# Interleaved products behind the LayerNorms, the conditioning row's Silu in memory, and two squares on VectorE in a two-layer diffusion step

## The chip, the cores and the metric

The kernel runs on one core of a Trainium2 chip. A core has TensorE (PE, the matmuls; PEld are its weight loads), VectorE (DVE), ScalarE (ACT), GpSimd (POOL) and SyncE (SP, which mostly starts DMAs). Each has its own instruction queue and works through it in order; semaphores between the queues hold an instruction back until its operands are there. What counts is the time of one execution on the device, in microseconds (us).

## The reference

Two layers, each a half-step SwiGLU FFN, a token mixer and another half-step FFN; the mixer is neighbourhood attention in layer 0 and a Hyena long convolution in layer 1. There are 640 tokens (128 of context, 512 latent), 1024 channels and 2816 hidden channels in an FFN. Every sub-layer is modulated from a conditioning vector and ends with a LayerNorm:

```
def modulate(x, shift, scale):
    return x * (1.0 + scale) + shift

def swiglu(h, w_in, w_out):
    g, u = jnp.split(h @ w_in, 2, axis=-1)
    return (jax.nn.silu(g) * u) @ w_out

def trunk_layer(x, cond, ...):
    sh1, sc1, g1, ... = jnp.split(jax.nn.silu(cond) @ mod_w_i + mod_b_i, N_MOD, axis=-1)
    x = layer_norm(ALPHA * x + 0.5 * g1 * swiglu(modulate(x, sh1, sc1), ...), ...)
    mix, extras = mixer(modulate(x, sh2, sc2))
    x = layer_norm(ALPHA * x + g2 * mix, ...)
    x = layer_norm(ALPHA * x + 0.5 * g3 * swiglu(modulate(x, sh3, sc3), ...), ...)
```

## The kernel before, in words

The six sub-layers are stages 0 to 5, and each has the LayerNorm of its number at its end: FFN 0, attention, FFN 1, FFN 2, Hyena, FFN 3. So LayerNorm 0 leads to attention, 1 to FFN 1, 2 to FFN 2, 3 to Hyena, 4 to FFN 3, and 5 to the output. x lies in memory with channels on partitions, as eight row blocks (dt or k, 0 to 7) of 128 channels by 640 tokens; the tokens are two chunks, c = 0 and c = 1, of CH = 320.

Products are made in fp32r with every operand split in a high and a low part (xh and xl, wh and wl): a row block takes three matmuls of 320 columns, a product over eight row blocks 24. A chunk's modulated row block is made by ACT (xm, L362), its high part by DVE (L386) or ACT (L388), its low part by DVE (L390).

`norm_steps` is a LayerNorm of one chunk, a generator in four steps: mean over channels by matmuls with a constant (mu, L401 and L403); its copy for POOL (mus, L405); subtraction on DVE, or on POOL for dt 2, 5 and 7 (L411), and squares (sq, L413); their mean (va, L420), square root and reciprocal (rq, L425 and L426) and its spread over partitions (rx, L428); the product that brings it to all rows (rs, L432); and last the multiplication of every row block (L436) with its modulation. The LayerNorm of chunk 0 runs inside the last products of its stage. That of chunk 1 is pending when they end: `tick()`, which the product helpers call after every fourth row block, takes it one step on at the 1st, 3rd, 4th and 6th tick (TICK_IN), and `settle()` finishes it. So the products with which the next stage starts on chunk 0 lie between its steps.

An FFN (`ffn`) starts with its plain products (`do_plain(f, c)`, two for each f: gate z = 0 and value z = 1; FIRST names the first three pairs (f, z)): f = 0 and 1 of chunk 0, then `settle()`, then the same for chunk 1. Each product is emitted whole, row block after row block. Then Silu on ACT (sg, L584), the multiplication (L572) and the split of the hidden row block (hh, hl). All later f are made by `do_fast(f)`, a seven-product scheme on four quarter blocks of the weights, whose sums s1 to s4 (L593 to L596, 128x512) are made on DVE for the first such f of an FFN and on POOL for the others. `combine_blocks` and `combine_rest` make the combined operands t1 to t5 for it from chunks 0 and 1 on DVE and ACT. `rescale` applies a LayerNorm's gain and bias to x on POOL (L477), 16 row blocks behind the first fast ones.

Attention starts with value products v0_5 and v0_0 and the query product qk0_0_0, Hyena with three of its input products, again each product as a whole.

`ffn_scope` loads the conditioning row for each FFN (condw, broadcast to 128 partitions by four DMAs) and applies Silu to it on ACT (L496); DVE uses it (L247) while it makes modulation vectors of later stages out of streamed weights.

Instructions are written in program order, and a scheduler then reorders them per engine by its own model of the times, within the dependences and the pools' buffers; `pin` keeps those that are passed through it in their written order. PSUM is in pools: two banks "mm", one "md", five "f" during an FFN. The name of a tile with its numbers, such as f2_0_0_1, is FFN 2, f = 0, c = 0, z = 1; mu2_1 is the mean of LayerNorm 2, chunk 1; s2_3_0 is the first sum of f = 3 in FFN 2.

## Time and profile before

| | |
|---|---|
| runs, median (lowest to highest) | 2799.68 us (2796.84 to 2804.33), 3 runs |
| the profiled execution | 2800.67 us |
| its span, first to last instruction | 2798.9 us |
| PE busy | 2683.2 us, 96% |
| DVE busy | 2111.8 us, 75% |
| ACT busy | 1196.1 us, 43% |
| POOL busy | 991.4 us, 35% |
| matmuls | 19404 |

The profile is of one execution, whose own time is 1.0 us above the median of the runs; 1.8 us of it lie outside the span. A busy matmul is modelled, and matmuls overlap: one of 320 columns is shown with 0.31 us, and the next one starts 0.15 us later when the clock is at its full level. The granted clock (PEclk) is 1.00 at 2.4 GHz and 0.50 at 1.2 GHz; a value between in a stretch is a mean of the two.

### The profile page before, as it was taken

How to read it: one execution, taken by the hardware profiler on the slowest of the kernel's cores; microseconds unless marked ns; L12 is line 12 of the kernel's file. 1: busy time of each engine (PE TensorE's matmuls, PEld its weight loads, DVE VectorE, ACT ScalarE, POOL GpSimd, SP SyncE). 2: the span in 40 equal slices, each digit the busy share in tenths (PEclk: the TensorE clock that was granted, in tenths of full speed). 3: DMA queues.
4: the chain of work that ended last, by engine and by line, in shares of the span. 5: the costliest groups of instructions: out<-in, count | busy, mean ns of one | idle time of the engine just before them, and what ended most of it. 6: DMA issues, size and time to landing. Idle time of an engine off the chain costs nothing.

```text
span 2798.9 us, 51125 instructions
## 1 busy us (share of the span) xinstructions
PE 2683.2 (96%) x19404; PEld 2558.2 (91%) x19404; DVE 2111.8 (75%) x4778; ACT 1196.1 (43%) x2572; POOL 991.4 (35%) x811
## 2 busy tenths in 40 slices
PE   7999999999999989999999999999999998999998
PEld 6898999989999688999989899998999987999997
DVE  5797888865765688888878888886777777765765
ACT  5662432444444462424346243344433336443433
POOL 4442533440000143534425354344223234543542
PEclk9999999999999999999999999999999998999999
DMA  8623324312222523243231332332423331322321
GB/s 281 236 95 98 126 91 129 114 56 90 77 74 74 191 73 128 84 129 129 84 106 63 112 128 91 121 121 67 132 84 106 101 100 35 99 76 76 98 68 54
DMA packets 111134, 293.45 MB, mean 105 GB/s; under 512 B 13823, under 2 KB 28927, under 8 KB 110760
## 3 DMA queue, kind: packets, MB, share of 16 engines
q1 hardware_dynamic: 107576, 285.80, 31.7%
q0 software_dynamic: 2304, 4.20, 0.5%
q8 instruction: 153, 2.51, 0.4%
q14 instruction: 93, 0.76, 0.1%
q10 hardware_dynamic: 1008, 0.19, 0.1%
HBM read 275.98 MB, written 14.16 MB: 104 GB/s over the span
## 4 chain that ended last, share of the span: by engine, by line
PE 67%; DVE 17%; DMA 6%; issue 4%; ACT 3%; POOL 3%; DVEq 0%; ACTq 0%; POOLq 0%; SPq 0%
PE f L527 8%; PE f L528 8%; PE f L529 8%; PE o L527 5%; PE o L528 5%; PE o L529 5%; DVE junk L247 5%; DMA mh<-in_modt 3%; DVE wl L158 3%; PE hy L343 2%; PE hy L342 2%; PE hy L344 2%; DVE xl L158 2%; PE qk L342 1%; PE qk L343 1%
## 5 line engine op out<-in xcount | busy, mean ns | idle before, releaser
L157 ACT CAST wh<-raw 128x512 fp32r<-128x512 f32 (+1 forms) x327 | 230.4, 709 | 302.5 <-PE o L528 151.9
L158 DVE TENSOR_TENSOR wl<-raw,wh 128x512 fp32r<-128x512 f32 (+1 forms) x274 | 274.6, 1003 | 70.1 <-ACT wh L157 69.3
L527 PE MATMUL f<-xh,wh 128*128 128x320 f32 x956 | 296.3, 314 | 15.7 <-DVE q L606 10.0
L528 PE MATMUL f<-xl,wh 128*128 128x320 f32 x956 | 297.5, 312 | 2.7 <-DVE xl L390 2.7
L529 PE MATMUL f<-xh,wl 128*128 128x320 f32 x956 | 294.7, 311 | 0.0
L247 DVE SCALAR_TENSOR_TENSOR junk<-mh,condw 128x256 f32<-128x256 f32 x576 | 267.1, 510 | 32.2 <-DMA mh<-in_modt 31.4
L527 PE MATMUL o<-hh,wh 128*128 128x320 f32 x840 | 261.0, 314 | 5.2 <-ACT hh L157 5.2
L528 PE MATMUL o<-hl,wh 128*128 128x320 f32 x840 | 259.1, 309 | 0.0
L529 PE MATMUL o<-hh,wl 128*128 128x320 f32 x840 | 258.1, 309 | 0.0
L353 DVE SCALAR_TENSOR_TENSOR x<-o,drv,x 128x320 f32<-128x320 f32 (+2 forms) x384 | 153.8, 434 | 105.3 <-PE o L529 104.7
L158 DVE TENSOR_TENSOR wl<-s,wh 128x512 fp32r<-128x512 f32 x187 | 170.9, 914 | 69.0 <-ACT wh L157 65.5
L157 ACT CAST wh<-s 128x512 fp32r<-128x512 f32 x187 | 115.8, 620 | 228.6 <-POOL s L594 69.3
L527 PE MATMUL f<-xh,xh 128*128 128x320 f32 x628 | 194.6, 314 | 8.1 <-DVE q L606 4.2
L593 POOL TENSOR_TENSOR s<-raw 128x512 f32<-128x512 f32 x73 | 110.7, 1516 | 256.2 <-DVE junk L247 167.3
L527 PEld LDWEIGHTS f<-xh,wh 128*128 128x128 f32 x956 | 180.0, 189 | 21.2 <-DVE q L606 12.1
L528 PE MATMUL f<-xl,xh 128*128 128x320 f32 x628 | 195.0, 311 | 0.2 <-DVE xl L390 0.2
L529 PE MATMUL f<-xh,xl 128*128 128x320 f32 x628 | 193.1, 310 | 0.0
L595 POOL TENSOR_TENSOR s<-raw,raw 128x512 f32<-128x512 f32 x73 | 106.5, 1459 | 238.6 <-DVE wl L158 150.2
L528 PEld LDWEIGHTS f<-xl,wh 128*128 128x128 f32 x956 | 180.8, 189 | 4.7 <-DVE xl L390 4.5
L527 PE MATMUL o<-hh,xh 128*128 128x320 f32 x568 | 178.2, 316 | 3.4 <-ACT hh L157 3.4
L529 PEld LDWEIGHTS f<-xh,wl 128*128 128x128 f32 x956 | 180.6, 189 | 0.0
L528 PE MATMUL o<-hl,xh 128*128 128x320 f32 x568 | 176.7, 312 | 1.2 <-DVE hl L158 1.2
(496 smaller groups left out, 8874.0 us busy)
## 6 DMA issues: line engine op xcount, KB each, us to landing
raw<-in_win SPq DMA_DIRECT2D x176, 512.0 KB, 3.6
raw<-in_wout SPq DMA_DIRECT2D x88, 512.0 KB, 4.3
mh<-in_modt SPq DMA_DIRECT2D x144, 256.0 KB, 2.9
raw<-in_modw SPq DMA_DIRECT2D x62, 512.0 KB, 4.8
raw<-in_hyin SPq DMA_DIRECT2D x24, 512.0 KB, 3.7
ksb<-kspec SPq DMA_DIRECT2D x40, 256.0 KB, 2.7
kspec<-ks SPq DMA_DIRECT2D x32, 256.0 KB, 3.2
raw<-in_wqk SPq DMA_DIRECT2D x16, 512.0 KB, 3.5
```

The source lines that it names most:

```text
L157: act.copy(pair[0], src)
L158: (eng or dve).tensor_tensor(pair[1], src, pair[0], ALU.subtract)
L247: dve.scalar_tensor_tensor(junk, raw[:, 256 * g:256 * g + 256], 1.0, condw[0][:, z], ALU.mult, ALU.mult, accum_out=acc[:, g0 + g, t, z:z + 1])
L342: te.matmul(ps, wh[:, i, cols], kh(k), start=(i == 0), stop=False)
L343: te.matmul(ps, wh[:, i, cols], kl(k), start=False, stop=False)
L344: te.matmul(ps, wl[:, i, cols], kh(k), start=False, stop=(i == n - 1))
L353: dve.scalar_tensor_tensor(x[:, dt, sl], ps[:, o], drv[:, st, 2, dt, z:z + 1], x[:, dt, sl], ALU.mult, ALU.add)
L527: te.matmul(ps, wh, kh, start=(first and i == 0), stop=False, skip_group_check=True)
L528: te.matmul(ps, wh, kl, start=False, stop=False, skip_group_check=True)
L529: te.matmul(ps, wl, kh, start=False, stop=(last and i == n - 1), skip_group_check=True)
L593: eng.tensor_tensor(s1, a21, a22, ALU.add)
L595: eng.tensor_tensor(s3, a11, a21, ALU.subtract)
```

## The change

Five things change. First, `interleaved` emits three products together, row block by row block, each in a bank of its own, with a tick behind every row block (eight ticks instead of two for each product). It is used for the first three products of each chunk in an FFN (`plain_pair` takes the place of `do_plain` for f = 0 and 1; the fourth product of the chunk follows as a whole), for v0_5, v0_0 and qk0_0_0 in attention, and for the first three products of Hyena. Second, the conditioning row gets its Silu once at the start and goes to a DRAM row, condd; `ffn_scope` loads that, and its Silu goes. Third, the squares of dt 6 and 7 are made on DVE. Fourth, banks: the LayerNorm of chunk 1 takes md behind stages 0 and 3, `ln_bank` (va from mm, the rest from md) behind 1, 2 and 4, and f behind 5. Fifth, the sums of the first fast f stay on DVE in FFN 0 only; in FFN 1, 2 and 3 they go to POOL with the others.

```diff
--- before.py
+++ after.py
...
+SQDVE = (6, 7)
...
+    def ln_bank(name):
+        return mm_bank(name) if name.startswith("va") else md_bank(name)
...
+    condd = dr.tile([4, 512], F32, name="condd")
+    crow = tmp("crow", 512, 4)
+    act.dma_start(out=crow, in_=a["condw"])
+    act.activation(crow, crow, AF.Silu)
+    act.dma_start(out=condd, in_=crow)
...
+    def interleaved(items):
+        for k in range(KD):
+            for ps, operands in items:
+                (sh, sl), (mh, ml) = operands(k)
+                for i, (s_, m_) in enumerate(((sh, mh), (sh, ml), (sl, mh))):
+                    te.matmul(ps, s_, m_, start=(k == 0 and i == 0), stop=(k == KD - 1 and i == 2),
+                              skip_group_check=True)
+            tick()
...
-                act.activation(sq, x[:, dt, sl], AF.Square)
+                if dt in SQDVE:
+                    dve.tensor_tensor(sq, x[:, dt, sl], x[:, dt, sl], ALU.mult)
+                else:
+                    act.activation(sq, x[:, dt, sl], AF.Square)
...
-                         in_=a["condw"][q:q + 1].broadcast_to([32, 512]))
-        act.activation(cw, cw, AF.Silu)
+                         in_=condd[q:q + 1].broadcast_to([32, 512]))
...
+            def plain_pair(c):
+                for key in FIRST + ((1, 1),):
+                    if key not in plain:
+                        plain[key] = uget(("win", idx) + key)
+                x_ = xb(range(KD), c)
+                ps = [fbank(f"f{idx}_{f}_{c}_{z}") for f, z in FIRST]
+                interleaved([(b, lambda k, u=plain[key]: (block(u, k), x_[k])) for b, key in zip(ps, FIRST)])
+                ps.append(fbank(f"f{idx}_1_{c}_1"))
+                product(ps[3], plain[(1, 1)], 0, x_)
+                for f in range(2):
+                    sg = tmp(f"sg{idx}_{f}_{c}", CH)
+                    act.activation(sg, ps[2 * f], AF.Silu)
+                    hidden(f, c, sg, ps[2 * f + 1], dve)
...
-                    b = mm_bank(f"f{idx}_{f}_{c}_{z}")[:, :CH] if (idx, f, c) == (0, 0, 0) else fbank(f"f{idx}_{f}_{c}_{z}")
+                    b = fbank(f"f{idx}_{f}_{c}_{z}")
...
-                eng = dve if f == NPLAIN[idx] else pool
+                eng = dve if idx == 0 and f == NPLAIN[idx] else pool
...
-                for f, c in [(0, 0), (1, 0), (0, 1), (1, 1)] + [(f, c) for f in range(2, NPLAIN[idx]) for c in range(2)]:
-                    if (f, c) == (0, 1):
-                        settle()
-                        t3 = combine_blocks(st)
-                    do_plain(f, c)
+                plain_pair(0)
+                settle()
+                t3 = combine_blocks(st)
+                plain_pair(1)
+                for f in range(2, NPLAIN[idx]):
+                    for c in range(2):
+                        do_plain(f, c)
...
-                pending.append(LayerNorm(1, st, md_bank if (st + 1) % 3 == 1 else fbank, nsum, TICK_IN))
+                pending.append(LayerNorm(1, st, fbank if st == 5 else md_bank if st % 3 == 0 else ln_bank, nsum, TICK_IN))
...
-            pending.append(LayerNorm(1, st, bank, nsum, TICK_IN))
+            pending.append(LayerNorm(1, st, ln_bank, nsum, TICK_IN))
...
-            values(0, wv, 5)
-            values(0, wv, 0)
             w0 = qk_slab(0, 0)
-            qk_gemm(0, 0, 0, w0)
...
+            bv = [mm_bank(f"v0_{slot}")[:, :256] for slot in (5, 0)]
+            bq = sc_bank("qk0_0_0")[:, :CH]
+            xh0, xl0 = xkh(0), xkl(0)
+            interleaved([(bv[0], value_operands(0)), (bv[1], value_operands(CTX + HD)),
+                         (bq, lambda k: ([t[:, k, :] for t in w0], (xh0(k), xl0(k))))])
...
-                first = [chunk(item, 0, w, mm_bank if i < 2 else hy_bank) for i, (item, w) in enumerate(head)]
+                first = [(mm_bank if i < 2 else hy_bank)(f"hyf{i}")[:, :CH] for i in range(3)]
+                xh0, xl0 = xkh(0), xkl(0)
+                interleaved([(b, lambda k, w=w: ([t[:, k] for t in w], (xh0(k), xl0(k))))
+                             for b, (_, w) in zip(first, head)])
```

Three places of the resulting order, all behind LayerNorm 2. PE, the first products of FFN 2, before; f2_0_0_0 is the product for f = 0, chunk 0, z = 0, s1_1 the sum over row blocks that the mean starts from:

```order
L527 MATMUL f2_0_0_0_16565<-xh_112,wh0_102 128x320
L528 MATMUL f2_0_0_0_16565<-xl_113,wh0_102 128x320
L529 MATMUL f2_0_0_0_16565<-xh_112,wl0_103 128x320
L527 MATMUL f2_0_0_0_16565<-xh_112,wh0_102 128x320
L528 MATMUL f2_0_0_0_16565<-xl_113,wh0_102 128x320
L529 MATMUL f2_0_0_0_16565<-xh_112,wl0_103 128x320
L401 MATMUL mu2_1_16578<-s1_1_115,mean_w_83 128x320
L403 MATMUL mu2_1_16578<-x_111,mean_w_83 128x320
L527 MATMUL f2_0_0_0_16565<-xh_112,wh0_102 128x320
L527 MATMUL f2_0_0_1_16607<-xh_112,wh1_104 128x320
```

The same place on PE now:

```order
L381 MATMUL f2_0_0_0_16573<-xh_117,wh0_107 128x320
L381 MATMUL f2_0_0_1_16574<-xh_117,wh1_109 128x320
L381 MATMUL f2_0_0_0_16573<-xl_118,wh0_107 128x320
L381 MATMUL f2_0_0_0_16573<-xh_117,wl0_108 128x320
L381 MATMUL f2_0_0_1_16574<-xl_118,wh1_109 128x320
L381 MATMUL f2_0_0_1_16574<-xh_117,wl1_110 128x320
L381 MATMUL f2_0_0_0_16573<-xh_117,wh0_107 128x320
L381 MATMUL f2_0_0_1_16574<-xh_117,wh1_109 128x320
L381 MATMUL f2_1_0_0_16575<-xh_117,wh2_111 128x320
L381 MATMUL f2_1_0_0_16575<-xl_118,wh2_111 128x320
L381 MATMUL f2_1_0_0_16575<-xh_117,wl2_112 128x320
L419 MATMUL mu2_1_16585<-s1_1_120,mean_w_83 128x320
```

Before, one product had PE for four row blocks, then came mu2_1, then the rest of the product. Now two, then three products share a row block, and the first of mu2_1's passes stands between matmuls of the second row block.

DVE at the end of chunk 0's chain, before; xm_5_0 to xm_7_0 are modulated row blocks, s_3_0 and s_3_1 the first two sums of the first fast f, the rows with mu_1 the subtractions for chunk 1:

```order
L390 TENSOR_TENSOR xl<-xm_5_0_16428,xh 128x320
L386 CAST xh<-xm_6_0_16434 128x320
L593 TENSOR_TENSOR s_3_0_17085<-raw_101 128x512
L390 TENSOR_TENSOR xl<-xm_6_0_16434,xh 128x320
L386 CAST xh<-xm_7_0_16440 128x320
L594 TENSOR_TENSOR s_3_1_17086<-s_3_0_17085,raw_100 128x512
L390 TENSOR_TENSOR xl<-xm_7_0_16440,xh 128x320
L411 TENSOR_TENSOR x<-x,mu_1_16578 128x320 x5
```

The same place on DVE now:

```order
L408 TENSOR_TENSOR xl<-xm_5_0_16431,xh 128x320
L404 CAST xh<-xm_6_0_16437 128x320
L408 TENSOR_TENSOR xl<-xm_6_0_16437,xh 128x320
L404 CAST xh<-xm_7_0_16443 128x320
L429 TENSOR_TENSOR x<-x,mu_1_16585 128x320 x2
L408 TENSOR_TENSOR xl<-xm_7_0_16443,xh 128x320
L429 TENSOR_TENSOR x<-x,mu_1_16585 128x320 x3
L432 TENSOR_TENSOR sq_1_6_16644<-x 128x320
L432 TENSOR_TENSOR sq_1_7_16647<-x 128x320
L447 RECIPROCAL rq_1_16674<-rq_1_16674 128x80
```

POOL behind the mean of LayerNorm 2, chunk 1, now, where the sums s_3_0 to s_3_3 of that f stand between the subtractions (mus_1) and the rescales (lng, lnb), and ahead of those of the next f:

```order
L627 TENSOR_TENSOR s_3_0_17088<-raw_106 128x512
L429 TENSOR_TENSOR x<-x,mus_1_16588 128x320 x3
L628 TENSOR_TENSOR s_3_1_17089<-s_3_0_17088,raw_105 128x512
L498 TENSOR_SCALAR x<-x,lng,lnb 128x320 x12
L629 TENSOR_TENSOR s_3_2_17090<-raw_105,raw_106 128x512
L498 TENSOR_SCALAR x<-x,lng,lnb 128x320 x4
L630 TENSOR_TENSOR s_3_3_17091<-raw_105,s_3_1_17089 128x512
L627 TENSOR_TENSOR s_4_0_17223<-raw_104 128x512
```

The two sums have left DVE's chain, two subtractions stand ahead of the last low part, and two squares come behind the last subtraction. On POOL the fourth sum stands behind all sixteen rescales.

ACT from the end of the squares of chunk 1, before; rq_1 is the square root, sg_0_0 the first Silu of FFN 2 (ACT_TABLE_LOAD is put in front of it by the compiler), xk the modulated row blocks of chunk 1:

```order
L413 ACTIVATE sq_1_7_16647<-x 128x320
L425 ACTIVATE rq_1_16677<-va_1_16620,eps_t 128x80
L584 ACT_TABLE_LOAD
L584 ACTIVATE sg_0_0_16682<-f_0_0_0_16565 128x320
L157 CAST hh_0_16553<-sg_0_0_16682 128x320
L362 ACTIVATE xk_0_16715<-x,drv 128x320
L362 ACTIVATE xk_1_16718<-x,drv 128x320
L388 CAST xh<-xk_0_16715 128x320
L362 ACTIVATE xk_2_16721<-x,drv 128x320
L388 CAST xh<-xk_1_16718 128x320
L362 ACTIVATE xk_3_16726<-x,drv 128x320
```

The same place on ACT now:

```order
L434 ACTIVATE sq_1_5_16641<-x 128x320
L446 ACTIVATE rq_1_16674<-va_1_16620,eps_t 128x80
L371 ACTIVATE xk_0_16700<-x,drv 128x320
L371 ACTIVATE xk_1_16703<-x,drv 128x320
L406 CAST xh<-xk_0_16700 128x320
L371 ACTIVATE xk_2_16706<-x,drv 128x320
L406 CAST xh<-xk_1_16703 128x320
L371 ACTIVATE xk_3_16711<-x,drv 128x320
L606 ACT_TABLE_LOAD
L606 ACTIVATE sg_0_0_16778<-f_0_0_0_16573 128x320
L606 ACTIVATE sg_1_0_16783<-f_1_0_0_16575 128x320
```

The table load and the first Silu have moved from ahead of the first four modulated row blocks to behind them, with the second Silu right behind.

## Rows read from the trace of the kernel before

**Rows 1.** The page, part 1: busy us (share of the span) xinstructions.

```profile
PE 2683.2 (96%) x19404; PEld 2558.2 (91%) x19404; DVE 2111.8 (75%) x4778; ACT 1196.1 (43%) x2572; POOL 991.4 (35%) x811
```

**Rows 2.** Waits of PE: who waited for whom: total us, times, longest.

```profile
PE f L527 <- ACT sg L584: 5.2, 4, 1.5
```

**Rows 3.** Windows behind LayerNorms 1, 2, 4, 3; columns in the first line.

```profile
core 0: us, PE busy (x) PEld busy (x) DVE busy (x) ACT busy (x) POOL busy (x), PEclk, DMA share, GB/s
989.50:1013.30 23.80, 23.24 (x169) 19.58 (x170) 14.42 (x36) 13.97 (x32) 4.34 (x6) 0.81 0.03 12
1454.00:1480.80 26.80, 22.81 (x170) 19.09 (x169) 18.60 (x38) 13.23 (x29) 6.99 (x7) 0.87 0.15 52
2337.80:2359.50 21.70, 21.69 (x169) 18.79 (x170) 13.98 (x35) 14.45 (x32) 4.33 (x6) 0.87 0.00 1
1923.90:1944.70 20.80, 15.97 (x145) 12.92 (x143) 13.65 (x33) 9.16 (x24) 12.73 (x19) 0.99 0.47 146
```

**Rows 4.** Timeline of PE behind LayerNorm 2; columns as in the first line.

```profile
start us, us, engine line op out<-in xcount [idle before <-releaser]
1458.41 0.41 PE L527 MATMUL f<-xh,wh 128*128 128x320 f32 x1 [1.14 <-DVE xh L386]
...
1476.74 0.70 PE L432 MATMUL rs<-rx,mean_w 128*128 128x320 f32 x2
```

**Rows 5.** Timeline of DVE, the same stretch.

```profile
1460.95 0.48 DVE L390 TENSOR_TENSOR xl<-xm,xh 128x320 fp32r<-128x320 f32 x1
...
1462.62 0.69 DVE L593 TENSOR_TENSOR s<-raw 128x512 f32<-128x512 f32 x1 [0.95 <-DMA raw<-in_win]
...
1464.57 1.36 DVE L594 TENSOR_TENSOR s<-s,raw 128x512 f32<-128x512 f32 x1
1465.85 1.15 DVE L390 TENSOR_TENSOR xl<-xm,xh 128x320 fp32r<-128x320 f32 x1
...
1474.38 0.49 DVE L428 TENSOR_TENSOR rx<-rq,qmask 128x320 f32<-128x320 f32 x1
...
1479.66 0.71 DVE L390 TENSOR_TENSOR xl<-xk,xh 128x320 fp32r<-128x320 f32 x1 [0.89 <-ACT xh L388]
```

**Rows 6.** Timeline of ACT, the same stretch.

```profile
1467.44 3.09 ACT L413 ACTIVATE sq<-x 128x320 f32<-128x320 f32 x8 [4.00 <-DVE x L411]
1473.26 0.33 ACT L425 ACTIVATE rq<-va,eps_t 128x80 f32<-128x80 f32 x1 [2.73 <-PE va L420]
1473.61 1.28 ACT L584 ACT_TABLE_LOAD   x1
```

**Rows 7.** Timeline of POOL, the same stretch and the fast block behind it.

```profile
1463.52 3.14 POOL L411 TENSOR_TENSOR x<-x,mus 128x320 f32<-128x320 f32 x3 [7.21 <-ACT mus L405]
...
1496.50 9.65 POOL L477 TENSOR_SCALAR x<-x,lng,lnb 128x320 f32<-128x320 f32 x4 [3.98 <-ACT tb L362]
1506.12 1.52 POOL L593 TENSOR_TENSOR s<-raw 128x512 f32<-128x512 f32 x1
```

**Rows 8.** Timeline of DVE at that fast block: a sum, and a split.

```profile
1497.39 0.68 DVE L596 TENSOR_TENSOR s<-raw,s 128x512 f32<-128x512 f32 x1
...
1506.41 1.58 DVE L158 TENSOR_TENSOR hl<-sg,hh 128x320 fp32r<-128x320 f32 x1
```

**Rows 9.** Timelines of ACT, DVE, PE ahead of rs, LayerNorm 4.

```profile
2329.99 1.28 ACT L425 ACT_TABLE_LOAD   x1
...
2333.26 0.69 DVE L593 TENSOR_TENSOR s<-raw 128x512 f32<-128x512 f32 x1 [0.97 <-DMA raw<-in_win]
...
2334.41 1.43 PE L432 MATMUL rs<-rx,mean_w 128*128 128x320 f32 x2 [4.21 <-DVE rx L428]
```

**Rows 10.** Timeline of ACT at the end, LayerNorm 5.

```profile
2784.37 3.09 ACT L413 ACTIVATE sq<-x 128x320 f32<-128x320 f32 x8 [0.62 <-DVE x L411]
```

**Rows 11.** Timeline of PE: LayerNorm 0's va, LayerNorm 3's rs, chunk 1.

```profile
599.52 0.62 PE L420 MATMUL va<-sq,mean_w 128*32 128x80 f32 x24 [0.95 <-DVE x L411]
...
1941.74 0.78 PE L432 MATMUL rs<-rx,mean_w 128*128 128x320 f32 x2 [1.82 <-DVE rx L428]
```

More of the change, by code (lines that the diff above doesn't have):

```diff
@@ L775, in values, with values_out @@
                     return
-                b = b[:, :256]
+                values_out(g, slot, b[:, :256])
+            def values_out(g, slot, b):
+                vhg, vlg = vh[g % 2][:, slot], vl[g % 2][:, slot]
                 if slot == 5:
@@ L790, in qk_gemm, with qk_out @@
             def qk_gemm(pr, z, c, w):
+                b = mm_bank(f"qk{pr}_{z}_{c}")[:, :CH]
+                gemm(b, w[0], w[1], range(KD), slice(0, P), xkh(c), xkl(c))
+                qk_out(pr, z, c, b)
+            def qk_out(pr, z, c, b):
                 th, tl = qk[(pr, z)]
                 s = 0.125 if z == 0 else 1.0
-                b = mm_bank(f"qk{pr}_{z}_{c}")[:, :CH]
-                gemm(b, w[0], w[1], range(KD), slice(0, P), xkh(c), xkl(c))
                 act.activation(th[:, CSL[c]], b, AF.Copy, scale=s)
@@ L963, in attention, with value_operands @@
             wv = values_load(0)
-            values(0, wv, 5)
-            values(0, wv, 0)
             w0 = qk_slab(0, 0)
-            qk_gemm(0, 0, 0, w0)
+            def value_operands(s0):
+                return lambda k: ([t[:, k, s0:s0 + P] for t in (xh, xl)], [w[:, k % 4, :] for w in wv[k // 4]])
+            bv = [mm_bank(f"v0_{slot}")[:, :256] for slot in (5, 0)]
[3 more added lines that the diff above has]
+                         (bq, lambda k: ([t[:, k, :] for t in w0], (xh0(k), xl0(k))))])
+            values_out(0, 5, bv[0])
+            values_out(0, 0, bv[1])
+            qk_out(0, 0, 0, bq)
             settle()
```

## The prediction

> **What bounds the kernel now.** I read the profile's page first. TensorE (PE) is busy 96% of the span and VectorE (DVE) 75% [rows 1]: the matmuls set the time, and what can be won is PE's idle time and the time that it runs at its lower clock. The list of waits came next: PE's waits are short and spread; one kind that the change touches is a bank that a Silu still reads, 5.2 us in four waits [rows 2]. Then I cut out the stretches behind the LayerNorms with the table of windows [rows 3]. In the one from LayerNorm 2 to the second half of FFN 2, PE is busy 22.81 of 26.80 us at a mean granted clock of 0.87; with levels of 2.4 and 1.2 GHz that is about 7 us at the lower one, which costs 3.5 us of full-speed work, so 4.0 + 3.5 = 7.5 us are lost there. The same sum gives 0.6 + 4.5 = 5.1 us behind LayerNorm 1, 0 + 2.8 behind LayerNorm 4, and 4.8, nearly all idle, behind LayerNorm 3. The timeline of PE shows how the loss arises: one product follows the row blocks of chunk 0 one by one and waits for DVE, 1.14 us at one block, and rs of chunk 1 comes at 1476.74 [rows 4].
>
> **The change part by part.** I take each stage end by itself, since the limits differ.
>
> *LayerNorm 2 to FFN 2, the largest term.* Before, one product's three matmuls per row block are all that PE has while DVE delivers, with mu of chunk 1 behind the first twelve. Now three products have nine matmuls per block. DVE's delivery itself gets shorter: two of the first fast block's sums stand in it, one with 0.95 us of wait for its DMA and 0.69 of work, one of 1.36, and a neighbouring xl takes 1.15 us where others take 0.48 [rows 5]. On POOL they are out of the way: 0.95 + 0.69 + 1.36 + 0.67 = 3.7 us off DVE ahead of the subtractions for chunk 1. The squares are next. ACT starts them at 1467.44 and needs 3.09 us for eight, to 1470.5 [rows 6]; with two on DVE it has six, 2.3 us. But POOL subtracts the mean from three row blocks, in 3.14 us [rows 7], and now has a sum ahead of them that can wait for the same DMA, so the last square cannot start much before 1467, and I take the squares done at 1467.5: 3.0 us earlier. From rq to the end of rx it is 1.6 us [rows 5, 6], but rx ended at 1474.87 and rs began at 1476.74 only, since rs stood behind matmuls of chunk 0 in PE's order. These are done earlier now, so up to 1.9 us of that go too: rs comes 3.0 to 4.9 us earlier, and with PE's chase ahead by another half a microsecond of clock I take 5.5 as the most and 4.5 as likely. Behind rs nothing covers the way to the first operands any more: before, DVE's first xl of chunk 1 began 2.9 us after rs [rows 4, 5] under a product of 24 matmuls; now five matmuls are left, and PE waits about 2.5 us. So PE gets at most 7.5 - 2.5 = 5.0 us. DVE is the other limit, since it is busy without a gap in the second half. Ahead of rs stood ACT's table load (1.28 us [rows 6]), the first Silu and DVE's two steps on it; they stand behind rs now, so DVE has 2 x 0.48 = 1.0 us more there, less two sums of 0.68 each [rows 8] that went to POOL, 1.4. From 4.5 that gives 4.9 without contention, and 2.7 if each of these two sums stretches one DVE instruction by 1.1 us: 1.58 for 0.48, as beside the POOL sum that began at 1506.12 [rows 7, 8]. I take **4.0**, between the two, a little nearer the uncontended end since POOL stands idle for 4 us ahead of its last rescales [rows 7] where one of the sums fits; ends 2.5 and 6.5 (the upper with the 5.5 and one bank wait of 1.2 gone).
>
> *LayerNorm 1 to FFN 1.* The same edit, but the two sums here wait for nothing, and the clock is low during the chase. PE: 5.1 us lost, minus the uncovered 2.5, minus what stays slow until the clock rises (an estimate of 5.5 us at half speed, 2.7): nothing is left. DVE's own chain saves its two sums and gains the two steps on the first Silu. **+0.5**, ends -1.5 and +3.
>
> *LayerNorm 4 to FFN 3.* PE waits 4.21 us for rs of chunk 0. Ahead of it stand ACT's table load (1.28 us), needed because condw's Silu had changed the table, and on DVE a sum that waits 0.97 us for a DMA and works 0.69, right ahead of rx [rows 9]. With the Silu kept in memory the load goes, and the sum goes to POOL. Together that is 2.9, but DVE's weight splits stand between and fill part of it, so rs comes about 1.5 us earlier. Later the gap moves as above (2.8 lost at the lower clock against 2.5 uncovered). **+1.5**, ends 0 and 3.
>
> *LayerNorm 3 to Hyena.* PE waits 1.82 us for rs of chunk 1 [rows 11]. Two squares fewer on ACT (3.09/8 = 0.39 us each) bring rs 0.8 us forward; the three products already share the row blocks. **+1**, ends 0 and 2.
>
> *LayerNorm 0 to attention.* PE waits 0.95 us ahead of va [rows 11]; more matmuls per block can fill that. But behind rs the two value products of chunk 1 now follow each other, and what was won waits there for DVE. **0**, ends -1 and +1.
>
> *FFN 0.* The three banks end together, so their Silus follow each other; a bank wait like those of today, at most 1.5 us [rows 2], may come or go. **0**, ends -1 and +1.
>
> *The end.* Behind the last product all is one chain, with eight squares in 3.09 us [rows 10]. Two on DVE take 0.77 us off ACT and stand beside it: **+0.6**, ends 0.3 and 0.8.
>
> *condw in memory.* ACT waits for its DMA at the start of FFN 1, 2 and 3, but PE waits there for DVE or a weight DMA, so that is worth nothing except for the table load counted above. At the start ACT has one small Silu more, beside the loading that PE waits for: 0.
>
> The sum is 4.0 + 0.5 + 1.5 + 1 + 0 + 0 + 0.6 = 7.6 us. The profiled execution took 2800.67 us, so it would take 2793.1; the median of the runs is 1.0 us below the profiled one, which makes **2792**. Runs of this kernel can tell about 0.3%, 8.4 us, from no change; the forecast lies just inside that.
>
> The page "SBUF — State Buffer" of the Trainium skill, section "Who interferes with whom", says that a DVE instruction with two SBUF inputs and a GpSimd one that reads SBUF cannot run at once: the later one waits in full. The trace agrees, with 1.58 us beside a POOL sum for what takes 0.48 alone. It speaks against this change, since it would hold for all twelve sums that move and for the two squares of each LayerNorm; the fourth rival is this rule at work.
>
> **The rivals.** *1. Given back.* The fast block's fourth sum stands behind all sixteen rescales on POOL in FFN 2 and 3. Beside a busy DVE the last four of these took 9.65 us, to 1506.15 [rows 7]; DVE did this sum itself at 1497.39 [rows 8]. DVE's split of that sum then waits, with all that is queued behind it, the combined blocks' and the hidden rows' splits, and PE waits for those. Then the starts of FFN 2 and 3 win nothing: 0.5 + 1 + 0.6 = 2.1, so 2797.6. Against it: a DVE that waits leaves POOL alone, and the rescales get shorter, so that the loss limits itself.
>
> *2. It does not do what it says.* The scheduler mixes products already, and behind LayerNorm 0 and 3 operands, not order, set PE's waits. If that holds for the FFNs, only the table load and the squares are left: 1.5 + 1 + 0.6 = 3.1, 2796.6.
>
> *3. PE-limited.* All FFN starts reach their upper ends: 6.5 + 3 + 3 + 1 + 0.6 = 14.1, and attention 1 more, 15.1: 2784.6. For it: PE is the bound overall and DVE has a quarter of the span in reserve [rows 1]. Against it: not in the second halves of the LayerNorms.
>
> *4. Slower.* POOL's sums stretch DVE: twelve sums, each 1.1 us more for a neighbour against 0.6 saved, 6.0 us lost, where DVE is the bound. The lower ends of the terms add up to -1 + 0 - 1.5 + 2.5 - 1 + 0 + 0.3 = -0.7, so the profiled time is 2800.7 + 6.7 = 2807.4 and the median 2806.4. It decides where DVE's delivery of chunk 1, and not PE, ends the start of an FFN in all three of them.
>
> **How the numbers follow.** Forecast 0.45, rival 1 0.17, rival 2 0.08, rival 3 0.16, rival 4 0.14. The forecast's own terms reach from 2784 to 2800; with rivals 3 and 4 the range is 2781 to 2807. Faster by over 0.3% means below 2791.3: rival 3 and a good two fifths of the forecast, 0.35. Slower by over 0.3% means above 2808.1: rival 4 where it comes out a little worse, 0.09. Within: 0.56.
>
> **What would show it.** In FFN 2 the chase should keep PE busy at a clock near 1, its DVE stretch should have no sums, and rs of chunk 1 should follow the first product by about 4.5 us less than before; PE's idle time should then stand in one piece behind rs. Behind LayerNorm 4 there should be no table load ahead of rq, and rs of chunk 0 should wait 2.7 instead of 4.2 us. If DVE instructions beside POOL's sums take 1.5 us in numbers, and DVE has no gap until the first fast block, rivals 1 or 4 hold. The forecast is wrong if rs of chunk 1 in FFN 2 moves by less than 3 us, or if the clock falls in the new gap behind it.

## The result: 18 us slower

The changed kernel took 2816.22 us (median of 4 runs, 2814.87 to 2821.85), the kernel before 2798.26 (4 runs, 2793.55 to 2804.33): a ratio of 1.0070, 95% interval 1.0057 to 1.0084. The forecast was 2792 and its range ended at 2807, so both the sign and the range were missed. The profiled execution, the slowest of the four, took 2821.85 us with a span of 2820.1, 21.2 above the span before. Each kernel is compared with the kernel before as it ran beside it (medians of 2798.3 to 2799.8 us); the ratios are those on record, and differ by up to 0.1% from the quotient of two medians.

The page of the changed kernel, part 1, answers to [rows 1]: no engine's share of the span has grown. PE makes the same 19404 matmuls, so its 13.0 us more of busy time go with a lower clock (0.979 in the mean of this execution, 0.985 before); DVE has 24 squares more and 12 sums less, and is busy for 10.4 us more.

```profile
PE 2696.2 (96%) x19404; PEld 2569.7 (91%) x19404; DVE 2122.2 (75%) x4790; ACT 1180.0 (42%) x2543; POOL 989.7 (35%) x823
```

The waits of PE after (who waited for whom: total us, times, longest). Two kinds are new: the first products of FFN 1 to 3 wait for a high part made by ACT, and FFN 0's first one for DVE. Waits for a bank that a Silu still reads are 2.3 + 1.7 = 4.0 us, no more than the 5.2 before [rows 2].

```profile
PE f L381 <- ACT xh L406: 6.8, 3, 2.4
...
PE f L381 <- DVE ks L1223: 2.4, 1, 2.4
PE f L547 <- ACT sg L606: 2.3, 3, 1.0
...
PE f L381 <- ACT sg L606: 1.7, 3, 0.6
```

The starts of FFN 1, 2 and 3 are best cut at rs. Timelines of PE before and then after, rs of chunk 0 and of chunk 1 (for FFN 2 before, the second is in [rows 4], 1476.74; for FFN 3 before, the first is in [rows 9], 2334.41):

```profile
985.88 1.29 PE L432 MATMUL rs<-rx,mean_w 128*128 128x320 f32 x2
...
1009.20 0.70 PE L432 MATMUL rs<-rx,mean_w 128*128 128x320 f32 x2
...
1447.26 0.70 PE L432 MATMUL rs<-rx,mean_w 128*128 128x320 f32 x2
...
2355.40 0.70 PE L432 MATMUL rs<-rx,mean_w 128*128 128x320 f32 x2
```

```profile
994.72 1.14 PE L453 MATMUL rs<-rx,mean_w 128*128 128x320 f32 x2
...
1018.85 0.70 PE L453 MATMUL rs<-rx,mean_w 128*128 128x320 f32 x2
...
1461.55 0.70 PE L453 MATMUL rs<-rx,mean_w 128*128 128x320 f32 x2
...
1487.50 0.81 PE L453 MATMUL rs<-rx,mean_w 128*128 128x320 f32 x2 [0.94 <-DVE rx L449]
...
2349.74 1.43 PE L453 MATMUL rs<-rx,mean_w 128*128 128x320 f32 x2 [3.24 <-DVE rx L449]
...
2372.73 0.70 PE L453 MATMUL rs<-rx,mean_w 128*128 128x320 f32 x2
```

From rs to rs it was 23.32, 29.48 and 20.99 us, and is 24.13, 25.95 and 22.99: +0.8, -3.5, +2.0. From rs of chunk 1 to the end of the plain products (the last is one for f = 2, chunk 1) it was 33.85 us in each FFN, and is 37.31, 37.25 and 37.59, together 10.6 more, though in each FFN 24 matmuls (3.5 us) that stood there have gone ahead of rs (23 in FFN 1). That second half is where the time went. It looks like this behind LayerNorm 4; PE after:

```profile
2372.73 0.70 PE L453 MATMUL rs<-rx,mean_w 128*128 128x320 f32 x2
2375.65 0.42 PE L381 MATMUL f<-xh,wh 128*128 128x320 f32 x1 [2.22 <-ACT xh L406]
2376.40 0.41 PE L381 MATMUL f<-xl,wh 128*128 128x320 f32 x1 [0.33 <-DVE xl L408]
...
2377.49 0.64 PE L381 MATMUL f<-xl,wh 128*128 128x320 f32 x1 [0.38 <-DVE xl L408]
...
2379.23 0.64 PE L381 MATMUL f<-xh,xh 128*128 128x320 f32 x1 [0.58 <-ACT sg L606]
```

And in windows of the same stretch (columns as in [rows 3]), after and then before:

```profile
2372.70:2376.70 4.00, 1.45 (x7) 0.71 (x6) 2.35 (x6) 2.45 (x5) 1.64 (x3) 1.00 0.00 0
2376.70:2380.70 4.00, 3.04 (x11) 2.38 (x10) 3.66 (x10) 3.89 (x7) 0.96 (x3) 0.57 0.02 4
2380.70:2384.70 4.00, 4.00 (x18) 4.00 (x18) 3.87 (x9) 4.00 (x11) 2.91 (x4) 0.58 0.00 0
2372.70:2410.30 37.60, 33.10 (x197) 31.17 (x196) 34.95 (x65) 29.08 (x66) 20.20 (x20) 0.91 0.10 29
```

```profile
2355.40:2389.30 33.90, 32.67 (x222) 32.25 (x221) 32.43 (x64) 26.66 (x62) 23.45 (x18) 1.00 0.11 32
```

Before, PE idles 1.2 us in this half at a clock of 1.00. After, it idles 4.5, mostly in the pieces above, and runs 8 us at 0.57 and 0.58, which costs 0.43 x 4 + 0.42 x 4 = 3.4 us of full-speed work. ACT shows why a bank is waited for (the 0.58 us): the table load, 1.28 us, and the first two Silus now stand between the modulated row blocks of chunk 1, where before they were over ahead of rs (a Silu at 2353.70).

```profile
2377.45 1.28 ACT L606 ACT_TABLE_LOAD   x1
2378.74 0.77 ACT L606 ACTIVATE sg<-f 128x320 f32<-128x320 f32 x2
```

These starts make 0.8 - 3.5 + 2.0 + 10.6 = 9.9 of the 21.2 us. The rest is about 1.5 us ahead of rs of chunk 0 behind LayerNorm 4, 3.0 behind LayerNorm 0 (from rs of chunk 0 to the end of the value products), 1.9 at the start of FFN 0, 2 at a late fast block of FFN 0 (a DVE wait for a weight DMA that p1 and x10, below, don't show), and 2.9 that is left over, spread over the long stages. In p1 and x10, which start FFN 0 in the same way, all of FFN 0 is no longer than before (by -0.1 and -0.4 us to rs of LayerNorm 0), so the 1.9 is not shown to last.

### The profile page after: what moved, and what is told of

Same layout as the page of the kernel before. It is cut to its first block, busy times and chain, and to the rows that moved or that the text cites. A ratio compares the mean times of both kernels' runs of the same rounds, so it can differ in the third digit from the quotient of the medians.

```text
span 2820.1 us, 51118 instructions
## 1 busy us (share of the span) xinstructions
PE 2696.2 (96%) x19404; PEld 2569.7 (91%) x19404; DVE 2122.2 (75%) x4790; ACT 1180.0 (42%) x2543; POOL 989.7 (35%) x823
## 4 chain that ended last, share of the span: by engine, by line
PE 65%; DVE 18%; DMA 5%; issue 4%; ACT 4%; POOL 3%; ACTq 0%; DVEq 0%; POOLq 0%; SPq 0%
PE f L547 7%; PE f L548 7%; PE f L549 7%; DVE junk L256 5%; PE o L547 5%; PE o L548 5%; PE o L549 5%; DVE wl L167 3%; DMA mh<-in_modt 3%; DVE xl L167 2%; PE hy L352 2%; PE hy L351 2%; PE hy L353 2%; PE f L381 2%; POOL s L630 2%
## 5 line engine op out<-in xcount | busy, mean ns | idle before, releaser
L547 PE MATMUL f<-xh,wh 128*128 128x320 f32 x828 | 257.4, 312 | 10.5 <-DVE q L640 8.9
L548 PE MATMUL f<-xl,wh 128*128 128x320 f32 x828 | 256.8, 310 | 0.0
L549 PE MATMUL f<-xh,wl 128*128 128x320 f32 x828 | 255.0, 310 | 0.0
L547 PE MATMUL f<-xh,xh 128*128 128x320 f32 x564 | 175.1, 311 | 8.9 <-DVE q L640 7.5
L549 PE MATMUL o<-hh,xl 128*128 128x320 f32 x568 | 175.4, 311 | 0.0
L547 PE MATMUL f<-t,wh 128*128 128x320 f32 x560 | 173.0, 310 | 2.4 <-DVE q L646 2.3
L548 PE MATMUL f<-xl,xh 128*128 128x320 f32 x564 | 174.0, 309 | 0.0
L549 PE MATMUL f<-xh,xl 128*128 128x320 f32 x564 | 173.4, 309 | 0.0
L548 PE MATMUL f<-t,wh 128*128 128x320 f32 x560 | 172.6, 309 | 0.0
```

Source lines behind the costliest of these rows:

```text
L547: te.matmul(ps, wh, kh, start=(first and i == 0), stop=False, skip_group_check=True)
L548: te.matmul(ps, wh, kl, start=False, stop=False, skip_group_check=True)
L549: te.matmul(ps, wl, kh, start=False, stop=(last and i == n - 1), skip_group_check=True)
```

## Experiments

Theories, as they arose: (A) the interleaved order costs by itself; (B) POOL's sums stretch DVE, rival 4 of the prediction; (C) the Silu in memory and the squares cost; (D) the LayerNorm's new banks let rs of chunk 1 fall behind all plain matmuls of chunk 0, so that nothing covers the way from rs to the first operands; (E) the first Silu comes after rs, with its table load, and holds banks that the products of chunk 1 need.

### The change taken apart

p1_interleave_alone is the changed kernel without Silu in memory, squares on DVE and sums on POOL:

```diff
-SQDVE = (6, 7)
+SQDVE = ()
...
-                         in_=condd[q:q + 1].broadcast_to([32, 512]))
+                         in_=a["condw"][q:q + 1].broadcast_to([32, 512]))
+        act.activation(cw, cw, AF.Silu)
...
-                eng = dve if idx == 0 and f == NPLAIN[idx] else pool
+                eng = dve if f == NPLAIN[idx] else pool
```

> The changed kernel with the Silu, the squares and the sums put back, so the kernel before plus the interleaving with its banks. Theory A (the interleaving is what costs: it leaves rs of chunk 1 behind nearly all matmuls of chunk 0 and then has nothing to cover the way to chunk 1's operands, and it starts FFN 0 in a bank that is not free yet): 14 to 22 us slower than the kernel before, near the changed kernel's 18. Theory B (the sums on POOL stretch VectorE): 4 us or less slower. Theory C (the Silu and the squares shift the chain): 4 us or less slower.

Measured 2816.77 (4 runs), ratio 1.0066 [1.0045, 1.0088]: the whole loss is in the interleaving and its banks, as far as runs of this kernel can tell.

p2_silu_squares and p3_sums_pool put the other parts into the kernel before: the Silu in memory with `SQDVE = (6, 7)`, and the sums:

```diff
-                eng = dve if f == NPLAIN[idx] else pool
+                eng = dve if idx == 0 and f == NPLAIN[idx] else pool
```

> The kernel before plus the Silu in memory and the two squares on VectorE alone. Theory A: 1 to 3 us faster, from the table load ahead of LayerNorm 4 and the shorter end. Theory B: the same. Theory C: 8 us or more slower.

> The kernel before plus the sums of the first fast block of FFN 1, 2 and 3 on POOL alone. Theory A: within 2 us of the kernel before. Theory B: 6 us or more slower, with VectorE instructions of 1.3 to 1.6 us beside the sums. Theory C: within 2 us.

Measured 2797.51, 0.9994 [0.9981, 1.0008], and 2799.06, 0.9999 [0.9988, 1.0011]: B and C fall. The stretch that B is made of is there, in the timelines of POOL and DVE after, in FFN 1:

```profile
1000.65 1.34 POOL L627 TENSOR_TENSOR s<-raw 128x512 f32<-128x512 f32 x1 [13.66 <-DMA raw<-in_win]
1002.07 1.27 POOL L628 TENSOR_TENSOR s<-s,raw 128x512 f32<-128x512 f32 x1
```

```profile
1002.10 1.59 DVE L408 TENSOR_TENSOR xl<-xm,xh 128x320 fp32r<-128x320 f32 x1
```

An xl takes 1.59 us beside a sum, as [rows 8] had it, yet the sums moved as a whole cost nothing that p3 can tell, and p1, which has them back on DVE, gets nothing back. The rule of the Trainium skill ("SBUF — State Buffer", "Who interferes with whom") holds for the instruction and says nothing of the sum.

p4_no_ffn_pairs keeps all but the interleaving in the FFNs: the loop over (f, c) with `do_plain` of before is put back. x6_attention_alone is the kernel before with the interleaving of attention (v0_5, v0_0, qk0_0_0) alone.

> The changed kernel with the FFN starts as before (whole products, with the new bank for FFN 0's first product) and all else as changed, attention's and Hyena's interleaving among it. Theory A: of the 18 us about 8 stay (3 in attention, up to 4 in FFN 0 by its bank, the rest at LayerNorm 1), so 2805 to 2808. Theory B: it stays near the changed kernel's time, 2812 or more.

> The kernel before with attention's first three products interleaved and nothing else. From the stages of the runs so far: from rs of LayerNorm 0, chunk 0, to the end of the values 2 to 3 us longer, and the whole 2 to 3 us slower. The rival, that the interleaving itself costs nothing there and the loss came with the other edits: within 1 us, and the stage no longer.

p4 2811.2, 1.0043 [1.0030, 1.0057]; x6 2799.37, 1.0001 [0.9987, 1.0016]. p4 lies between what A and B had forecast. So A can't be all: some 60% of the loss stay without interleaved FFN products. By its time, attention's interleaving can't be told from nothing, but its interval reaches 4.5 us.

### The LayerNorm's banks (D)

x5_banks_alone puts the new banks alone into the kernel before; x10_after_old_banks and x9_interleave_old_banks put the old ones into the changed kernel and into p1 (the same lines the other way round):

```diff
-                pending.append(LayerNorm(1, st, md_bank if (st + 1) % 3 == 1 else fbank, nsum, TICK_IN))
+                pending.append(LayerNorm(1, st, fbank if st == 5 else md_bank if st % 3 == 0 else ln_bank, nsum, TICK_IN))
-            pending.append(LayerNorm(1, st, bank, nsum, TICK_IN))
+            pending.append(LayerNorm(1, st, ln_bank, nsum, TICK_IN))
```

> The kernel before with one edit: the LayerNorm of chunk 1 takes its banks from mm and md behind stages 1, 2 and 4 as in the changed kernel, with no interleaving, Silu, squares or sums changed. In the resulting order rs of chunk 1 stands behind all 96 matmuls of chunk 0 (72 before) and none is left to cover the way to chunk 1's operands (24 before). Theory D (the banks cost, since a scarce f bank had held the fourth product back behind rs): 8 to 14 us slower, FFN 1 and FFN 3 each 3 to 6 us longer. Theory A (the interleaving costs): within 2 us of the kernel before.

> The changed kernel with the banks of chunk 1's LayerNorm as before, all else as changed; rs of chunk 1 stands behind 72 matmuls again and 24 are left for cover. Theory D: 10 to 14 of the 18 us come back, 2802 to 2806, what is left lying in attention and FFN 0. Theory A: 2812 or more.

> The interleaving in FFN, attention and Hyena with the banks of chunk 1's LayerNorm as before, and no Silu, squares or sums changed. Theory D: 2 to 6 us slower than the kernel before, from attention and FFN 0, with FFN 1 to 3 within 2 us of the kernel before or shorter. Theory A: 12 us or more slower.

x5 2804.1, 1.0009 [0.9995, 1.0023]; x10 2808.03, 1.0036 [1.0019, 1.0052]; x9 2812.85, 1.0048 [1.0031, 1.0065]. With old banks the changed kernel gets some 8 us back, p1 only 4, which the intervals hardly tell from nothing; alone the new banks cost little, not D's 8 to 14. x9 came out as A had it (12 us or more slower), x10 between A and D. In the order of PE's instructions the banks decide how many of the 96 plain matmuls of chunk 0 are left behind rs of chunk 1: 24 before, in x9 and x10; none in x5; one or none after. Before, the five f banks were taken by three products, mu and va, so the fourth product had to wait for va's bank and stood behind rs. D is a part, not the cause. PE in x10, behind the 24 matmuls, meets the next wait, for the Silu:

```profile
2366.28 0.41 PE L381 MATMUL f<-xh,wh 128*128 128x320 f32 x1 [2.29 <-ACT sg L606]
```

### The late first Silu (E)

y4_late_first_silu is the kernel before with one step moved, in FFN 1 to 3: Silu, multiplication and split of f = 0, chunk 0, come behind `settle()`. PE's order stays, with 24 matmuls behind rs.

```diff
+            late = []
...
-                sg = tmp(f"sg{idx}_{f}_{c}", CH)
-                act.activation(sg, ps[0], AF.Silu)
-                hidden(f, c, sg, ps[1], dve)
+                def finish():
+                    sg = tmp(f"sg{idx}_{f}_{c}", CH)
+                    act.activation(sg, ps[0], AF.Silu)
+                    hidden(f, c, sg, ps[1], dve)
+                if idx > 0 and (f, c) == (0, 0):
+                    late.append(finish)
+                else:
+                    finish()
...
                         settle()
+                        while late:
+                            late.pop(0)()
```

> The kernel before with one edit: in FFN 1, 2 and 3 the Silu, multiplication and split of f = 0, chunk 0 come behind settle() and not right behind their two products. PE's order stays (72 matmuls ahead of rs of chunk 1, 24 for cover); on ACT the table load and that Silu go from ahead of rs to behind the fourth modulated row block of chunk 1, as in the changed kernel. Theory E (this move, which interleaving forces since its three products end together, costs in the second half of the LayerNorm, where VectorE and ACT are the bound): from rs of chunk 1 to the end of f = 2 each of the three FFNs 2 to 3 us longer, the whole 5 to 9 us slower. Theory D (only the place of rs in PE's order matters): within 2 us of the kernel before.

2814.63 (4 runs), 1.0062 [1.0047, 1.0077], twice what E had forecast: this step alone, in the kernel before, loses nearly what the whole change loses. Its waits of PE and, behind LayerNorm 4, its timeline and the window of its second half:

```profile
PE f L527 <- ACT sg L587: 15.5, 10, 2.3
```

```profile
2371.33 0.42 PE L527 MATMUL f<-xh,wh 128*128 128x320 f32 x1 [2.29 <-ACT sg L587]
...
2390.17 0.41 PE L527 MATMUL f<-xh,wh 128*128 128x320 f32 x1 [1.00 <-ACT sg L587]
...
2398.92 0.41 PE L527 MATMUL f<-xh,wh 128*128 128x320 f32 x1 [1.45 <-ACT sg L587]
```

```profile
2364.80:2402.70 37.90, 33.16 (x222) 32.21 (x221) 35.54 (x69) 30.36 (x70) 21.22 (x18) 1.00 0.13 39
```

Before, this kind of wait was 5.2 us in four [rows 2]; 10.3 of the span's 13.5 us more are in it, at a clock of 1.00. PE waits with operands at hand for a bank that a Silu has yet to read.

y5_late_mult_only leaves the Silu in its place and moves only `hidden(...)`, the multiplication and split on DVE and ACT. z5_banks_and_late_silu is y4's edit on top of x5.

> The kernel before; of the first pair's hidden row block in FFN 1, 2 and 3 the Silu stays where it was (ACT, directly behind the square root of chunk 1's LayerNorm), and only the multiplication and the split move behind settle(). With the Silu moved too the loss was 15.8 us (2814.63). If the loss is ACT's (table load and Silu among the first modulated row blocks of chunk 1), it goes: 2798 to 2803. If it is the two PSUM banks that the late Silu and the late multiplication hold, one is now free in time: about half stays, 2804 to 2810. If it is DVE's work, two more steps of 0.5 us and more where DVE sets the pace: all of it stays, 2811 to 2816. I hold the banks for likeliest.

> The kernel before with the new banks of chunk 1's LayerNorm (alone 2804.1) and the late Silu, multiplication and split of the first pair (alone 2814.63). The new banks leave all five f banks to the products, four of chunk 0 and one free. If the late Silu costs by the banks that it holds, the free one covers part of it: 2804 to 2811. If it costs by ACT's or DVE's work behind rs, both losses stand: 2814 to 2822, the changed kernel's own time.

y5 2802.77 (12 runs), 1.0009 [0.9998, 1.0020]; z5 2808.15 (8 runs), 1.0031 [1.0019, 1.0044]. The late multiplication and split explain 2.5 (at most 5.6) of y4's 17 us, so E works through the Silu on ACT. And z5 loses half of what y4 does, although it has no cover behind rs: with the f banks free of the LayerNorm, PE's first wait for the Silu shrinks from 2.29 to 0.93 us.

```profile
2364.55 0.41 PE L530 MATMUL f<-xh,wh 128*128 128x320 f32 x1 [2.22 <-ACT xh L391]
...
2368.13 0.64 PE L530 MATMUL f<-xh,xh 128*128 128x320 f32 x1 [0.93 <-ACT sg L590]
```

So with the old banks the held bank is a large part. I had put y5 at 2804 to 2810 by it; at 2802.77 it lies where the expectation had ACT's work as the cause. Both go together if the gate's bank, which the Silu frees, is the one that counts, and the value's bank, which the multiplication frees, is hardly missed. How the loss divides between bank and ACT's 2.05 us of load and Silus stays open.

The changed kernel has the new banks, and there the late Silu costs in another way, and less: 6 us by z5 against x5, which differ by y4's edit alone. Windows from rs of chunk 1 to the end of the plain products in FFN 1, 2 and 3 (columns as in [rows 3]), x5, z5, and the changed kernel (its third is shown above, 2372.70:2410.30); each holds the same 192 matmuls, or one more:

```profile
1010.10:1044.30 34.20, 29.68 (x198) 28.65 (x197) 32.66 (x65) 25.81 (x60) 23.45 (x18) 1.00 0.11 32
1475.40:1509.10 33.70, 29.52 (x195) 28.66 (x196) 32.53 (x65) 26.18 (x61) 24.61 (x18) 1.00 0.11 33
2352.60:2386.80 34.20, 31.16 (x197) 30.13 (x197) 32.84 (x65) 26.59 (x63) 23.85 (x18) 0.95 0.10 32
```

```profile
1010.50:1048.50 38.00, 33.18 (x197) 31.25 (x196) 35.63 (x70) 29.63 (x68) 20.39 (x18) 0.91 0.11 32
1478.50:1514.60 36.10, 32.63 (x196) 31.15 (x197) 33.58 (x67) 28.66 (x65) 22.37 (x18) 0.91 0.15 42
2361.60:2398.00 36.40, 32.53 (x198) 31.18 (x197) 34.00 (x67) 28.87 (x66) 22.55 (x18) 0.91 0.15 44
```

```profile
1018.90:1056.20 37.30, 33.18 (x198) 31.03 (x197) 34.46 (x65) 29.66 (x67) 23.01 (x20) 0.91 0.14 40
1487.50:1524.80 37.30, 34.06 (x196) 32.22 (x197) 34.83 (x65) 29.05 (x66) 23.35 (x20) 0.86 0.10 29
```

PE idles 11.7 us in the three windows of x5, 12.2 in z5 and 11.9 after: the late Silu adds next to no waiting. The windows are 8.4 and 10.1 us longer than x5's because PE is busy that much longer with the same matmuls, at a lower clock. All three kernels have the gap of 2.2 us or more behind rs; in z5 and after it is followed by waits of 0.2 to 0.9 us for low parts and for the Silu, which x5 doesn't have there. That these are what the clock falls by is not shown.

z1_after_pair_silu is the changed kernel with only the two products of f = 0 interleaved and their Silu right behind them in the program:

```diff
-                ps = [fbank(f"f{idx}_{f}_{c}_{z}") for f, z in FIRST]
-                interleaved([(b, lambda k, u=plain[key]: (block(u, k), x_[k])) for b, key in zip(ps, FIRST)])
...
+                    ps = [fbank(f"f{idx}_{f}_{c}_{z}") for z in range(2)]
+                    if f == 0:
+                        interleaved([(b, lambda k, u=plain[(0, z)]: (block(u, k), x_[k])) for z, b in enumerate(ps)])
...
```

> The changed kernel, but only the two products of the first pair (f = 0) are interleaved, and the Silu, multiplication and split of that pair follow in the program right behind them; the other two products follow whole. All else as changed, the LayerNorm's banks too, so rs of chunk 1 still stands last. If the three-way ending of products is what costs, since it puts three banks and two Silus behind rs at once: 2799 to 2806. If the banks of the LayerNorm and the place of rs do: 2808 to 2816.

2813.05 (6 runs), 1.0046 [1.0030, 1.0062]: three products ending together are not needed. One matmul at most is left behind rs here, and the scheduler still puts the Silu behind the first modulated row blocks, so z1 doesn't part the place of rs from that of the Silu.

### What is worth keeping

y1_pair_only is the kernel before with only the two products of f = 0, chunk 0, interleaved in FFN 1 to 3. y3_silu_squares_sums2 is the kernel before with the Silu in memory, squares on DVE for chunk 1 and LayerNorm 5 only, and sums on POOL in FFN 2 only. y2_y3_and_pair is both.

```diff
+                if idx > 0 and c == 0 and f == 0:
...
+                    x_ = xb(range(KD), c)
+                    interleaved([(b, lambda k, u=plain[(f, z)]: (block(u, k), x_[k])) for z, b in enumerate(ps)])
...
-                act.activation(sq, x[:, dt, sl], AF.Square)
+                if dt in SQDVE and (c == 1 or st == 5):
+                    dve.tensor_tensor(sq, x[:, dt, sl], x[:, dt, sl], ALU.mult)
...
-                eng = dve if f == NPLAIN[idx] else pool
+                eng = dve if idx != 2 and f == NPLAIN[idx] else pool
```

> The kernel before with the two products of f = 0, chunk 0 alone interleaved in FFN 1, 2 and 3. In the resulting order rs of chunk 1 stands behind 48 matmuls and 48 are left as cover; the first Silu still comes behind rs. Theory D alone: rs of chunk 1 comes 2 to 3.5 us earlier in each FFN and the whole gets 4 to 10 us faster. Theory E: rs comes earlier by as much, but the second half gives it back, so the whole is within 3 us of the kernel before.

> No interleaving: the kernel before with the Silu in memory, the two squares on VectorE for chunk 1 and at the end only, and the first fast block's sums on POOL in FFN 2 only, where a sum on VectorE had waited for its DMA. By the stages of the runs so far 3 to 8 us faster than the kernel before, 2791 to 2796; if the gains of the Silu and squares alone and of the sums alone were one profile's scatter, within 2 us.

> The same with the pair of f = 0, chunk 0 interleaved as well. Theory D alone: another 4 us faster, 2787 to 2792. Theory E: no faster than without the pair.

y1 2798.57, 1.0001 [0.9988, 1.0014]; y3 2796.92, 0.9996 [0.9987, 1.0006]; y2 2794.73, 0.9986 [0.9975, 0.9997]. y2 beats both kernels, by 4 us against the one before; its interval only just leaves out 1, and of fifteen kernels tried one can come out so by chance. In y1 and y2 the first Silu is as late as in y4, but 48 matmuls (7 us) are left behind rs and cover it, with banks to hand. That is read from their traces; no run has the 48 without the interleaved pair. PE of y2 behind LayerNorm 4 waits ahead of rs, and then, in a window of the second half, not at all:

```profile
2347.82 1.03 PE L450 MATMUL rs<-rx,mean_w 128*128 128x320 f32 x2 [1.73 <-DVE rx L446]
```

```profile
2351.80:2386.00 34.20, 34.20 (x235) 34.20 (x235) 33.38 (x65) 27.53 (x63) 17.49 (x16) 1.00 0.13 35
```

The runs side by side; "left behind rs" counts plain matmuls of chunk 0 in PE's order in FFN 1 to 3, "Silu" is the place of the first one in ACT's order against the first four modulated row blocks of chunk 1:

| kernel | banks | left behind rs | Silu | ratio to before |
|---|---|---|---|---|
| before | old | 24 | ahead | 1 |
| x5 | new | 0 | ahead | 1.0009 |
| p4 | new | 0 | ahead | 1.0043 |
| z5 | new | 0 | behind | 1.0031 |
| z1 | new | 0 or 1 | behind | 1.0046 |
| p1, after | new | 0 to 6, 0 or 1 | behind | 1.0066, 1.0070 |
| y4 | old | 24 | behind | 1.0062 |
| x9, x10 | old | 24 | behind | 1.0048, 1.0036 |
| y1, y2 | old | 48 | behind | 1.0001, 0.9986 |

Every kernel with a late Silu is 9 to 20 us slower than before, but for those with 48 matmuls left. p4 doesn't fit: it differs from x5 by parts that alone can't be told from nothing (p2, p3, x6), and by Hyena's interleaving and FFN 0's first bank, which were not tried alone. Its 9 us are open.

The traces say where a part of them may lie. From rs of chunk 0 behind LayerNorm 0 to that behind LayerNorm 1 (402.80 us before), the seven kernels with interleaved attention (after, p1, p4, x6, x9, x10, z1) are 2.8 to 6.0 us longer, 4.1 in the mean, and the nine others -3.8 to 3.3, 0.2 in the mean. So attention's interleaving may well cost some 4 us, which x6's interval allows. Of the changed kernel's 20 us, the banks (2.5, x5), the late Silu with these banks (6, z5 against x5) and these 4 explain some 12, each give or take 4 or so; the rest is open.

## Why the prediction was wrong

**LayerNorm 2 to FFN 2 (+4.0).** The first half came as forecast, if smaller: from 1463.0 to 1489.8 PE runs at 1.00 where it had 0.87 [rows 3], and rs of chunk 1 comes 3.5 us earlier, against 4.5 forecast and 3 as the limit. The wait behind rs is 2.22 us, for the 2.5 forecast. The step that failed is "So PE gets at most 7.5 - 2.5 = 5.0 us": it charged the gap and nothing behind it. The last part of the prediction named the sign, a clock that falls in the new gap, and it fell (windows after, columns as in [rows 3]):

```profile
1463.00:1489.80 26.80, 24.16 (x206) 21.87 (x205) 19.85 (x44) 13.54 (x30) 9.35 (x9) 1.00 0.25 80
1489.80:1496.00 6.20, 4.79 (x14) 3.72 (x15) 5.08 (x12) 5.90 (x12) 2.92 (x6) 0.50 0.00 0
```

The second half ran at 0.86 (1487.50:1524.80, above), which costs up to 0.14 x 37.3 = 5.2 us; PE idles 3.2 us in it, 2.0 more than before, and 24 matmuls (3.5) have gone. That makes it 3.4 us longer, and the term 3.5 - 3.4, that is nothing.

**The first Silu.** The prediction saw it move behind rs, and charged DVE 1.0 us for it. y5 agrees with that size (2.5 us in three FFNs), and it is the small part. What it did not price is on ACT and in PSUM: the table load and two Silus in front of a high part that PE needs, and the gate's bank held until then. y4 puts that at 17 us with the old banks, as waits; z5 against x5 puts it at 6 with the new ones, as a lower clock, and the changed kernel's windows look like z5's.

**LayerNorm 1 to FFN 1 (+0.5)** was -4.3: 0.8 ahead of rs, 3.5 behind. **LayerNorm 4 to FFN 3 (+1.5)** was -7.2: the same 2.0 and 3.7 us around rs of chunk 1, and 1.5 at rs of chunk 0. Its table load went as forecast, but rs still waits 3.24 us instead of 2.7, since DVE, busy with weight splits, makes the two squares of chunk 0 late; PE waits for them twice. DVE and PE after:

```profile
2343.88 2.21 DVE L432 TENSOR_TENSOR sq<-x 128x320 f32<-128x320 f32 x2
```

```profile
2345.08 0.35 PE L441 MATMUL va<-sq,mean_w 128*32 128x80 f32 x8 [0.74 <-DVE sq L432]
2346.15 0.35 PE L441 MATMUL va<-sq,mean_w 128*32 128x80 f32 x8 [0.72 <-DVE sq L432]
```

The prediction asked what the squares take off ACT, not what stands ahead of them on DVE. In y3, with these two back on ACT, 1.0 of the 1.5 us is gone from the profile; rs then waits 4.06 us, with the table load gone and the sum still on DVE, so the load alone was worth 0.2 at most.

**LayerNorm 3 to Hyena (+1)**: rs of chunk 1 still waits 1.82 us; it comes 0.9 earlier, of which 0.2 is left at the next product. **Attention (0, ends -1 and +1)**: 3.0 us lost in the profile, 2.2 in x6's; x6's time doesn't show it, and doesn't exclude it. **FFN 0 (0)**: its first product takes an f bank, which the filter's spectrum phase held until then (PE waits 2.40 us for DVE); most of what that starts is given back by f = 2, and 1.9 stay in this profile. **The end (+0.6)**: six squares on ACT take 2.37 us instead of 3.09 [rows 10], but rq then waits 1.15 us for va instead of 0.61, 0.2 is left, and from rs to the end it takes 9.5 us instead of 9.2, so nothing is won. **condw (0)** stands, by p2.

**The rivals.** The sum of rival 4, 2806, came nearest, with a mechanism that p3 refutes. Rival 2 started from the scheduler, which mixes products already; here it also sets the order through the banks, which no rival looked at. The five changes were priced as if the banks were a detail of them. Three slips in the working bear little on this: the upper ends of the terms add up to 17.3 us, that is 2782 and not 2784; behind rs of chunk 1 one matmul of chunk 0 or none was left, not five; and the 5.5 us at half speed in the term for LayerNorm 1 stand on no row.

## What to carry to other kernels

When products are interleaved so that they end together, count what is left on PE behind the next dependent step, and which banks the consumers of the ended products still hold: a gap that moves is worth nothing if the cover and the banks don't move with it. Interleave as few products as fill the first gap, so that whole products remain behind it: two and not three with the old banks here (y1 and y2 against x9 and x10), while with the new banks two were little better (z1). Where a scheduler orders by free buffers, a change of banks is a change of order, and should be priced as one.

## What was not expected of the hardware

A gap of some 2.2 us on PE was followed by a lower clock after and in x10 (0.58 from 2367.5 to 2371.5), and by none in y4 (1.00 from 2364.8 on, with a wait of 2.29), nor in FFN 1 of x5 (1.00, with a wait of 2.54): the same wait had a different price, and no run here isolates why. The DVE instructions beside POOL's sums grew from 0.48 to 1.59 us, and two casts from 0.55 to 1.64, without a cost to the whole in p3. Switching ACT's table cost just the load's row of 1.28 us: the Silu began 1.29 us after the load did.
